# A fixed instruction order of a hybrid attention layer: half steps, evenly spaced scores, dense tiles dealt anew

## The chip, the cores and the metric

One core of a Trainium2 chip runs the whole layer in one launch. The metric is the device time of one execution in microseconds (us); 701.57 is the median of three for the kernel before (701.05 to 702.87).

## What is computed

One layer of a decoder on 512 prompt rows and 8 sample rows (one new token each, with 1024 cached rows in pages). The rows, modulated by an adaLN condition, are projected by `w_in` to all queries, keys, values and gates; two token mixers run on them, and their outputs are gated, projected up, merged, projected once more and normed. Cut to its core:

```python
h = x * (1.0 + scale) + shift
parts = split(h @ w_in)          # a_q a_kc a_vc a_ks a_vs a_kw a_vw a_g a_z b_q b_k b_v b_z m_a m_b
ck, cv = compress(k_cmp), compress(v_cmp)      # gelu(blk @ w1 + b1) @ w2 + b2, blocks of 32 rows, stride 16
o_a = g0 * attn(q, ck, cv) + g1 * attn(q, selected blocks) + g2 * attn(q, window of 512)   # NSA
o_b = attn(q, top 3 past blocks of 256 and the own block)                                 # MoBA
y_a = (o_a * silu(a_z)) @ w_up_a
y_b = (o_b * silu(b_z)) @ w_up_b
mixed = (sigmoid(m_a) * y_a + sigmoid(m_b) * y_b) @ w_out
x_new = layer_norm(alpha * x + gate * mixed)
```

The sample rows do the same over caches that a page table addresses: 64 pages each of the compression, selection and MoBA caches.

## The kernel before, in words

The projection by `w_in` is cut into **dense tiles** of 128 columns, named in `COLS` (q0 to q3 and bq0 to bq3 are queries, bk, bv, z, bz the other parts, `m0` to `m7` stand for the two tiles ma and mb of one merge gate). One tile (`dense`, line 538) loads a weight block of 512 KB, splits it into a high and a low part in two halves (ScalarE casts the high part, line 300; GpSimd or VectorE subtracts it, line 217; each half one step ahead of its use), and runs 48 matmuls of 260 columns into two PSUM banks called `d`. In the trace `d` is such a tile, `hl` a split weight, `raw` a loaded block, `s` a bank of scores, `p` probabilities, `pt` their transposes in PSUM, `pp` these copied back, `o` attention outputs, `e` the decode branch's bank.

The stages follow each other like this. To 52 us the adaLN condition and the first columns. Then the compression network of prompt and samples (`phi_prompt`, `phi_pair`, ends near 155 us; `u` its inputs, `gl` its gelu, line 781), with the tiles of `FILLS[0]` between; `dec_cmp`, the compression branch of the samples, with `CMP_FILLS` (to 170). Then the **prompt's attention**, eight pairs of heads (`attend`, pi = 0 to 7, 174 to 524 us), mixed with the samples' other branches (`dec_a`, `dec_b`) and with `FILLS[1]` to `FILLS[8]`; a stage with the rest of the samples' work and `FILLS[9]` (to 590); and the up and output projections with the norm.

The order is written by the kernel itself. Each of these works is a generator that yields an estimated cost; `merge` always steps the one with the smallest share of its total done. The totals are `ATT` (attention of a pair), `DEC_SHARE` and `DEC` (how far the samples' branches shall be behind each pair) and `fill_cost`. Where `behind[0]` is set, TensorE keeps exactly the order in which its instructions are written (`in_turn` ties each to the one before); the other engines are ordered by the tile scheduler, which honours `tc.high_priority()`.

One step of the attention handles one head's job (`step`, line 1111) as a list: for k = 0 to 3 a score of 512, 384, 256 or 128 columns (`score`), then a transposition of an earlier job (`turn`), at k = 1 the value product (`value`). A score is two matmuls and then a chain over three engines: VectorE adds the band and takes the extremum (1031, 1033), ScalarE takes the exponential (1036), VectorE the reciprocal (1037), GpSimd scales the probabilities (1038). Two banks `s` exist, so the third score waits for the first one's exponential. Items yield their estimated cost, so a step's scores stand as close together as the shares allow; a dense tile yields after every 12 matmuls.

The samples' branches read their caches through the ring `C` of two buffers (`CRAW = 2`) of 1 MB: the selection keys `slck` and MoBA's `mobk`, `mobv` page by page on SyncE's queue (line 729: read a page number, then one DMA), and the selection values `slcv` by two indirect DMAs a buffer on GpSimd (line 1160), 512 KB each.

Of the kernel before, what the change touches and what calls it, by code (L numbers as in the profile page):

```python
# [35 lines left out]
FILLS = [["ks", "vs", "ag", "vw", "q0", "kw", "q1", "q2", "q3"],  # L36
         ["bq1", "m0", "m1"],
         ["bk0", "bv0", "m2"],
         ["z0", "m3"],
         ["bv1", "z1", "m4"],  # L40
# [3 lines left out]
         ["bz1", "m5"],  # L44
         ["bz2", "m6", "g0", "g1", "bz3", "g2", "g3", "m7"]]
CMP_FILLS = ["bq2", "bq0", "bq3"]
DEC_SHARE = [0.13, 0.26, 0.39, 0.51, 0.57, 0.63, 0.765, 0.87]
DEC, DEC_PACE = 55100.0, 0.78
PHIS = 49353.58399999998
ATT = [17100] * 4 + [7100] * 3 + [11000]  # L50
# [113 lines left out]
def build(tc, A):  # L164
# [16 lines left out]
    def in_turn(i):  # L181

        D["pe"] = i
        if behind[0]:
            if behind[1] is not None:
                order(i, behind[1])
            behind[1] = i
        return i
# [33 lines left out]
    with ExitStack() as es:  # L222
# [315 lines left out]
        def dense(name, M=128):  # L538
# [3 lines left out]
            for hf in range(8 // per_u):  # L542
                hl = W.use()
                for bk in range(2):
                    for kk in range(per_u):
                        k = hf * per_u + kk
                        for j, (x, hb) in enumerate(((0, hTh), (1, hTh), (0, hTl))):
                            mm(acc[bk][:M, :HB], hl[:, x, kk * M:kk * M + M], hb[:, k, bk * HB:bk * HB + HB],
                               k == 0 and j == 0, k == 7 and j == 2)
                    if posts and (hf or bk):  # L550
                        posts.pop(0)()
                    yield per_u * 333
# [469 lines left out]
        def score(j, i):  # L1022
            n = 128 * i + 128
            s = p_s()
            for k in range(2):
                mm(s[:, :n], j.q2[k][:, i * 128:i * 128 + 128], j.kd[:, :n], k == 0, k == 1)
            sm = at.tile([128, 4], F32, name="sm", bufs=8)
# [10 lines left out]
            nc.gpsimd.tensor_scalar(pr, pr, sm[:, 3:4], j.gate(i), op0=OP.mult, op1=OP.mult)  # L1038
            return 2 * max(107, 0.42 * n)

        def turn(j, gi):
# [5 lines left out]
            if COPY_ENG[gi] == "a":  # L1047
                j.copied[gi] = nc.scalar.copy(t[:, :n], p[:, :n])  # L1048
            else:
                j.copied[gi] = nc.vector.tensor_copy(t[:, :n], p[:, :n])  # L1050
            return 109 * len(GRP[gi])
# [3 lines left out]
        def value(js):  # L1055
# [14 lines left out]
            return 160 + 1.7 * 1280 + (900 if last and pi < 4 else 0)  # L1070

        def finish(j):
            nc.scalar.mul(y[:, j.pi, :T], cur["o"], 0.5)
            return 1

        def cmp_score(r):
# [21 lines left out]
            return 8 * 200  # L1098

        def cmp_turn(r):  # L1100
# [6 lines left out]
            return 436  # L1107
# [3 lines left out]
        def step(j, extra=()):  # L1111

            extra = list(extra)
            b, a1, a0 = pipe
            seq = []
            for k in range(4):
                if j is not None:
                    seq.append((score, j, 3 - k))
                if b is not None and k:
                    seq.append((turn, b, k - 1))  # L1120
                if k == 1 and a1 is not None and a1.g:
                    seq.append((value, (a0, a1)))
                    if a1.last:
                        seq.append((finish, a1))
                if extra and k == 2:
                    f, arg = extra.pop(0)
                    seq.append((f, arg))
            pipe[:] = [j, b, a1]
            for f, *args in seq:
                yield f(*args)  # L1130
# [26 lines left out]
        def slcv_item(i):  # L1157
            def fn(t):
                for k in range(2):
# [42 lines left out]
        def dec_a():  # L1202

            xs = de.tile([128, 1026], F32, name="xs", tag="x")
# [150 lines left out]
        for pi in range(8):  # L1355
            fl = Flow(fills(FILLS[pi + 1]), fill_cost(FILLS[pi + 1]))
            if pi == 0:

                for _ in range(4):
                    fl.step()  # L1360
            merge(Flow(attend(pi), ATT[pi]), Flow(part(DEC_SHARE[pi]), max(1.0, (DEC_SHARE[pi] - done) * DEC)), fl)
            done = DEC_SHARE[pi]
        at_es.close()

# [8 lines left out]
        behind[:] = False, None  # L1373
# [375 lines left out]
```

## Time and profile before

| | us |
|---|---|
| median of the runs (701.05 to 702.87) | 701.57 |
| the profiled execution | 704.4 |
| its span, first to last instruction | 702.6 |
| TensorE busy (89% of the span) | 625.0 |
| VectorE, ScalarE, GpSimd busy | 322.9, 297.5, 288.4 |

The granted clock of TensorE is 0.938 of full speed over the span, and the DMA queues move 123.73 MB. TensorE is the busiest engine by far in every stage but the first, so a stage is read by what keeps TensorE idle, and by the clock that it was granted; busy time of the other engines counts only where TensorE waits for it.

### The profile page before, as it was taken

Reading aid. Unit: us, or ns where it says so; the run is one execution under the profiler, and the core shown is the slowest. Engines: PE = TensorE matmul, PEld = TensorE weight load, DVE = VectorE, ACT = ScalarE, POOL = GpSimd, SP = SyncE. Lnnn points to the kernel's source line nnn. Section 1 sums busy time; section 2 is a strip of 40 time slices with the busy share of each in tenths; the row PEclk is TensorE's granted clock in tenths of the full one; section 3 lists DMA queues with packets and bytes.
Section 4 is the critical chain, followed back from the end, with each engine's and each line's share of the span. In section 5 each row is a group of like instructions: output and inputs, shape, how many; then the busy total and the mean of one; then the engine's idle time right before and its main releaser. Section 6 shows DMA issues by size and latency. Waiting matters only on the chain. (4 is left out here: it accounts for less than half of the span.)

```text
span 702.6 us, 13239 instructions
## 1 busy us (share of the span) xinstructions
PE 625.0 (89%) x4709; PEld 519.6 (74%) x4709; DVE 322.9 (46%) x817; ACT 297.5 (42%) x678; POOL 288.4 (41%) x327
## 2 busy tenths in 40 slices
PE   5989999579599899999997898898989789999993
PEld 2788999579488767676675778775757569899773
DVE  3474365316655714734461636462321034655167
ACT  3375465325264635544451635452422142433422
POOL 2043847315253224434353535242402035566556
PEclk9999999689699999999998999989999879999997
DMA  8984476204447555666572653418779753244303
GB/s 313 393 304 140 139 196 181 61 30 126 130 140 260 202 158 173 210 226 213 165 244 71 225 203 113 136 37 281 234 240 304 269 203 105 72 150 132 139 1 122
DMA packets 63524, 123.73 MB, mean 176 GB/s; under 512 B 8354, under 2 KB 26594, under 8 KB 62946
## 3 DMA queue, kind: packets, MB, share of 16 engines
q1 hardware_dynamic: 62050, 118.69, 51.5%
q0 software_dynamic: 1408, 4.20, 1.8%
q8 instruction: 37, 0.61, 0.3%
q14 instruction: 29, 0.24, 0.1%
HBM read 113.81 MB, written 9.05 MB: 175 GB/s over the span
## 5 line engine op out<-in xcount | busy, mean ns | idle before, releaser
L172 PE MATMUL d<-hTh,hl 128*128 128x260 f32 (+1 forms) x1408 | 278.9, 296 | 6.7 <-ACT hl L300 4.9
L172 PEld LDWEIGHTS d<-hTh,hl 128*128 128x128 f32 (+1 forms) x1408 | 225.9, 195 | 29.1 <-issue 17.3
L172 PE MATMUL d<-hTl,hl 128*128 128x260 f32 (+1 forms) x704 | 204.4, 290 | 0.0
L172 PEld LDWEIGHTS d<-hTl,hl 128*128 128x128 f32 (+1 forms) x704 | 136.7, 194 | 0.5
L217 POOL TENSOR_TENSOR hl<-raw,hl 128x512 fp32r<-128x512 f32 x56 | 73.6, 1314 | 140.6 <-ACT hl L300 125.6
L300 ACT CAST hl<-raw 128x512 fp32r<-128x512 f32 (+1 forms) x111 | 68.0, 615 | 95.9 <-PE d L172 86.0
L217 DVE TENSOR_TENSOR hl<-raw,hl 128x512 fp32r<-128x512 f32 (+1 forms) x55 | 51.5, 936 | 75.8 <-ACT hl L300 67.8
L1036 ACT ACTIVATE p<-s,sm 128x512 f32<-128x512 f32 (+1 forms) x96 | 50.6, 528 | 53.8 <-DVE sm L1033 43.2
L1038 POOL TENSOR_SCALAR p<-p,sm,gp 128x512 f32<-128x512 f32 (+1 forms) x64 | 40.1, 630 | 78.0 <-DVE sm L1037 75.0
L191 PE MATMUL pt<-cst,p 128*128 128x128 f32 x240 | 40.8, 286 | 14.8 <-POOL p L1038 9.8
L172 PE MATMUL d<-yh,hl 128*128 128x260 f32 x256 | 46.3, 282 | 0.0
L191 PEld LDWEIGHTS pt<-cst,p 128*128 128x128 f32 x240 | 28.3, 146 | 22.5 <-POOL p L1038 11.9
L1033 DVE CUSTOM_DVE_ANT_0 s<-s,band 128x256 f32<-128x256 f32 (+1 forms) x48 | 17.4, 364 | 58.7 <-PE s L172 45.5
L172 PE MATMUL s<-kd,q 128*128 128x512 f32 (+1 forms) x96 | 36.4, 379 | 6.8 <-ACT p L1036 5.9
L172 PEld LDWEIGHTS d<-yh,hl 128*128 128x128 f32 x256 | 39.7, 188 | 1.1 <-issue 0.4
L1038 POOL TENSOR_SCALAR p<-p,sm,cst 128x512 f32<-128x512 f32 (+3 forms) x32 | 20.0, 626 | 40.9 <-DVE sm L1037 37.0
L172 PE MATMUL s<-u,w1h 128*128 128x256 f32 (+1 forms) x160 | 32.4, 298 | 4.1 <-ACT u L800 1.8
L172 PE MATMUL d<-yl,hl 128*128 128x260 f32 x128 | 36.0, 282 | 0.0
L172 PEld LDWEIGHTS s<-kd,q 128*128 128x128 f32 x96 | 19.2, 200 | 22.2 <-ACT p L1036 8.3
L172 PE MATMUL s<-kd,qx 128*128 128x512 f32 (+1 forms) x96 | 32.6, 339 | 0.0
L175 PE MATMUL o<-pp,v 128*64 128x384 f32 (+3 forms) x168 | 31.8, 448 | 0.0
L1048 ACT COPY pp<-pt 128x512 f32<-128x512 f32 (+1 forms) x48 | 23.0, 479 | 20.7 <-PE pt L191 20.3
(414 smaller groups left out, 1154.5 us busy)
## 6 DMA issues: line engine op xcount, KB each, us to landing
raw<-w_cols SPq DMA_DIRECT2D x46, 512.0 KB, 5.5
raw<-mobk SPq DMA_DIRECT2D x64, 256.0 KB, 3.9
raw<-mobv SPq DMA_DIRECT2D x64, 256.0 KB, 4.3
craw<-cmp SPq DMA_DIRECT2D x64, 128.0 KB, 2.7
u<-ada_ss SPq DMA_DIRECT2D x12, 512.0 KB, 9.1
raw<-slck SPq DMA_DIRECT2D x64, 64.0 KB, 2.0
raw<-ada_g SPq DMA_DIRECT2D x8, 512.0 KB, 4.2
raw<-w_up SPq DMA_DIRECT2D x8, 512.0 KB, 4.4
```

The source lines that it names most:

```text
L172: i = mmraw(out, lhsT, rhs, start=start, stop=stop, skip_group_check=True)
L175: i = mmraw(out, lhsT, rhs, start=start, stop=stop, skip_group_check=True)
L191: return in_turn(nc.tensor.transpose(out, x, unit))
L217: (nc.gpsimd if eng == "p" else nc.vector).tensor_sub(out, x, f32(hi))
L300: nc.scalar.copy(h, src)
L1033: nc.vector.tensor_tensor_reduce(out=s[:, b:n], in0=s[:, b:n], in1=j.band[:, 256 - (n - b):], scale=1.0, scalar=top, op0=OP.add, op1=OP.mi ...
L1036: nc.scalar.activation(pr, s[:, :n], AF.Exp, scale=-1.0, bias=sm[:, 1:2], accum_out=sm[:, 2:3])
L1038: nc.gpsimd.tensor_scalar(pr, pr, sm[:, 3:4], j.gate(i), op0=OP.mult, op1=OP.mult)
L1048: j.copied[gi] = nc.scalar.copy(t[:, :n], p[:, :n])
```

## The change

- `FILLS`: bq2, bq0 and bq1 go to the compression network's stage (three tiles more there); `CMP_FILLS` now holds bq3, bk0, bv0; m6 goes from the last stage to the attention's last pair. The attention has 26 tiles instead of 27, the last stage 4 instead of 6. `ATT`, `DEC`, `DEC_SHARE`, `DEC_PACE` get other numbers; the first pair's fill is run for 8 steps ahead instead of 4, each half as long.
- `dense` yields after every 6 matmuls instead of 12.
- `step` has four slots, each one score, one transposition and what else belongs there, and each slot yields the same cost, 1000.
- The chain behind a score (`probs`) and the copy of transposes get high priority.
- `slcv` gathers are issued only after the latest scaling of probabilities on GpSimd (`D["pool"]`).
- `dec_a` loads its first two buffers ahead.
- The fixed order ends with the attention; afterwards TensorE's instructions only stand behind the attention's last one (`floor`), and the scheduler orders them.

```diff
-FILLS = [["ks", "vs", "ag", "vw", "q0", "kw", "q1", "q2", "q3"],
-         ["bq1", "m0", "m1"],
-         ["bk0", "bv0", "m2"],
-         ["z0", "m3"],
-         ["bv1", "z1", "m4"],
+FILLS = [["ks", "vs", "ag", "vw", "q0", "bq2", "kw", "q1", "q2", "q3", "bq0", "bq1"],
+         ["m0", "m1"],
+         ["m2", "m3"],
+         ["z0", "bv1", "m4"],
+         ["z1", "m5"],
...
-         ["bz1", "m5"],
-         ["bz2", "m6", "g0", "g1", "bz3", "g2", "g3", "m7"]]
-CMP_FILLS = ["bq2", "bq0", "bq3"]
-DEC_SHARE = [0.13, 0.26, 0.39, 0.51, 0.57, 0.63, 0.765, 0.87]
-DEC, DEC_PACE = 55100.0, 0.78
+         ["bz1", "m6"],
+         ["bz2", "g0", "g1", "bz3", "g2", "g3", "m7"]]
+CMP_FILLS = ["bq3", "bk0", "bv0"]
+DEC_SHARE = [0.155, 0.28, 0.405, 0.53, 0.59, 0.645, 0.74, 0.855]
+DEC, DEC_PACE = 57600.0, 0.85
-ATT = [17100] * 4 + [7100] * 3 + [11000]
+ATT = [16000] * 4 + [8000] * 3 + [10400]
...
         D["pe"] = i
+        if "floor" in D:
+            order(i, D["floor"])
...
-                    if posts and (hf or bk):
-                        posts.pop(0)()
-                    yield per_u * 333
+                        if kk % 2 == 1:
+                            if posts and (hf or bk) and kk == per_u - 1:
+                                posts.pop(0)()
+                            yield 666
...
+            with tc.high_priority():
+                probs(j, i, n, s)
+
+        def probs(j, i, n, s):
...
-            nc.gpsimd.tensor_scalar(pr, pr, sm[:, 3:4], j.gate(i), op0=OP.mult, op1=OP.mult)
-            return 2 * max(107, 0.42 * n)
+            D["pool"] = nc.gpsimd.tensor_scalar(pr, pr, sm[:, 3:4], j.gate(i), op0=OP.mult, op1=OP.mult)
...
-            extra = list(extra)
             b, a1, a0 = pipe
-            seq = []
-            for k in range(4):
+            slots = [[] for _ in range(4)]
+            for k, seq in enumerate(slots):
                 if j is not None:
-                    seq.append((score, j, 3 - k))
+                    seq.append(lambda i=3 - k: score(j, i))
                 if b is not None and k:
-                    seq.append((turn, b, k - 1))
-                if k == 1 and a1 is not None and a1.g:
-                    seq.append((value, (a0, a1)))
-                    if a1.last:
-                        seq.append((finish, a1))
-                if extra and k == 2:
-                    f, arg = extra.pop(0)
-                    seq.append((f, arg))
+                    seq.append(lambda i=k - 1: turn(b, i))
+            if a1 is not None and a1.g:
+                slots[1].append(lambda: value((a0, a1)))
+                if a1.last:
+                    slots[1].append(lambda: finish(a1))
+            for f, arg in extra:
+                slots[2].append(lambda f=f, arg=arg: f(arg))
             pipe[:] = [j, b, a1]
-            for f, *args in seq:
-                yield f(*args)
+            for seq in slots:
+                for f in seq:
+                    f()
+                    yield (600 if j is None else 1000) / len(seq)
...
             def fn(t):
-                for k in range(2):
+                with tc.issue_after(D["pool"].ins):
+                  for k in range(2):
                     nc.gpsimd.indirect_dma_start(out=t[:, k * 1024:k * 1024 + 1024], out_offset=None, in_=A["slcv"],
...
         def dec_a():
 
+            C.load_to(1)
+            yield 2500
...
-                for _ in range(4):
+                for _ in range(8):
                     fl.step()
+                fl.total, fl.done = fl.total - fl.done, 0.0
...
         at_es.close()
+        behind[0] = False
+        D["floor"] = D["pe"]
...
-        behind[:] = False, None
+        D.pop("floor")
```

**TensorE, within the attention of one pair.** Before, a score of 512 columns, one of 384 and a transposition of four stand together (`s_3354`, `s_3364`, `pt_3374`):

```order
L172 MATMUL s_3354<-kd_1627,q2_2141 128x512
L172 MATMUL s_3354<-kd_1627,qx_2142 128x512
L172 MATMUL s_3364<-kd_1627,q2_2141 128x384
L172 MATMUL s_3364<-kd_1627,qx_2142 128x384
L191 MATMUL pt_3374<-cst0_72,p_3308 128x128
L191 MATMUL pt_3374<-cst0_72,p_3263 128x128
L191 MATMUL pt_3374<-cst0_72,p_3159 128x128
L191 MATMUL pt_3374<-cst0_72,p_3116 128x128
L172 MATMUL d_3278<-hTh_73,hl_3282 128x260 x2
L172 MATMUL d_3278<-hTl_74,hl_3282 128x260
```

In the changed order such three items, now with dense matmuls between score and score (`s_3410`, its 512 columns, stands six more rows of `d_3424` above this piece) and between score and transposition:

```order
L172 MATMUL d_3424<-hTh_73,hl_3328 128x260 x2
L172 MATMUL d_3424<-hTl_74,hl_3328 128x260
L172 MATMUL s_3443<-kd_1649,q2_2341 128x384
L172 MATMUL s_3443<-kd_1649,qx_2342 128x384
L172 MATMUL d_3425<-hTh_73,hl_3328 128x260 x2
L172 MATMUL d_3425<-hTl_74,hl_3328 128x260
L172 MATMUL d_3425<-hTh_73,hl_3328 128x260 x2
L172 MATMUL d_3425<-hTl_74,hl_3328 128x260
L193 MATMUL pt_3459<-cst0_72,p_3365 128x128
L193 MATMUL pt_3459<-cst0_72,p_3324 128x128
L193 MATMUL pt_3459<-cst0_72,p_3278 128x128
L193 MATMUL pt_3459<-cst0_72,p_3256 128x128
```

A quarter of a dense tile's work, 12 or 6 matmuls, now separates each item from the next.

**GpSimd, at the second pair of gathers.** Before, both gathers of the pair stand behind a weight split, wherever the scheduler found room:

```order
L217 TENSOR_TENSOR hl<-raw,hl 128x512
L1160 DMA raw<-slcv,vidx 128x1024 x2
L1038 TENSOR_SCALAR p<-p,sm,gp 128x512
L1038 TENSOR_SCALAR p<-p,sm,gp 128x384
L993 TENSOR_TENSOR qx<-y,q_4209 64x512
L1038 TENSOR_SCALAR p<-p,sm,gp 128x256
L1038 TENSOR_SCALAR p<-p,sm,gp 128x128
```

With the change each pair stands right behind a scaling of probabilities; the first and the second pair come within one job's four scalings, with the `qx` split (which waits for the first pair's landing) between:

```order
L1045 TENSOR_SCALAR p<-p,sm,gp 128x512
L1160 DMA raw<-slcv,vidx 128x1024 x2
L1045 TENSOR_SCALAR p<-p,sm,gp 128x384
L1045 TENSOR_SCALAR p<-p,sm,gp 128x256
L996 TENSOR_TENSOR qx<-y,q_4404 64x512
L1045 TENSOR_SCALAR p<-p,sm,gp 128x128
L1160 DMA raw<-slcv,vidx 128x1024 x2
L1045 TENSOR_SCALAR p<-p,sm,gp 128x512
```

**TensorE, where the second of these pairs is read.** The score of 128 columns whose scaling (the last `p` 128x128 above) releases the gathers, and the read `e<-raw,tp` of what they bring:

```order
L172 MATMUL s<-kd,q_3719 128x128
L172 MATMUL s<-kd,qx 128x128
L172 MATMUL e<-vnew,np 128x128 x2
L172 MATMUL d<-hTh,hl 128x260 x2
L172 MATMUL d<-hTl,hl 128x260
L172 MATMUL d<-hTh,hl 128x260 x2
L172 MATMUL d<-hTl,hl 128x260
L193 MATMUL pt<-cst_72,p 128x128 x2
L172 MATMUL e<-raw,tp 32x128
L175 MATMUL e<-raw,tp 32x128 x31
```

Between the score and the read stand two products of the new rows, six dense matmuls and two transposes. At the fourth pair it is six dense matmuls alone.

In the changed order the four reads of `slck` (`e<-raw,zn`) stand 27, 24 and 26 rows apart on TensorE, where before it was 29, 49 and 47; 24 dense matmuls, three scores, twelve transposes and one read lie between the first and the second.

## Rows read from the trace of the kernel before

**Rows 1.** Windows by stage: us of the stretch, busy time (instructions) of each engine, clock, DMA share, GB/s.

```profile
120.00:160.00 40.00, 27.41 (x184) 26.33 (x183) 11.36 (x22) 11.48 (x26) 11.13 (x13) 0.74 0.17 48
160.00:200.00 40.00, 32.29 (x221) 28.49 (x221) 22.68 (x68) 16.52 (x40) 15.97 (x18) 0.83 0.45 131
200.00:520.00 320.00, 292.27 (x2290) 230.50 (x2288) 149.65 (x471) 150.38 (x384) 125.68 (x149) 0.96 0.57 187
520.00:587.00 67.00, 59.62 (x433) 47.14 (x426) 15.97 (x16) 17.80 (x36) 18.92 (x18) 0.90 0.69 234
```

**Rows 2.** TensorE's waits: line waited for, us in total, times, longest us.

```profile
PE pt L172 <- ACT gl L781: 10.5, 2, 6.2
PE pt L191 <- POOL p L1038: 9.8, 7, 4.2
...
PE s L172 <- ACT p L1036: 7.2, 6, 2.1
...
PE d L172 <- ACT hl L300: 4.9, 2, 3.4
...
PE d L172 <- POOL hl L217: 1.8, 2, 1.0
```

**Rows 3.** Timeline of TensorE at 128 us, columns: start, us, what [idle before <- releaser].

```profile
128.05 0.58 PE L172 MATMUL pt<-gl,w2h 128*128 128x256 f32 x1 [6.16 <-ACT gl L781]
```

**Rows 4.** Windows of two stretches at half clock in the compression stage.

```profile
124.30:138.00 13.70, 7.83 (x33) 7.39 (x34) 5.12 (x7) 3.73 (x8) 4.74 (x6) 0.50 0.28 77
144.80:151.60 6.80, 6.24 (x28) 6.24 (x29) 0.79 (x3) 1.13 (x3) 0.00 (x0) 0.50 0.00 0
```

**Rows 5.** Chain of waits, 544 to 560 and 612 to 617 us: start, us, what.

```profile
546.42 0.55 PE e L172
...
557.38 0.63 ACT hl L300
...
558.08 1.27 POOL hl L217
...
615.12 1.43 PE d L172 x12
```

**Rows 6.** Timeline, SyncE's queue and TensorE, at 177 and 181 us.

```profile
176.80 23.53 SPq L729 DMA_DIRECT2D raw<-slck  x37
...
180.80 1.03 PE L172 MATMUL e<-raw,zn 128*32 128x512 f32 x1 [5.59 <-DMA raw<-slck]
```

**Rows 7.** Timeline of all engines, 357 to 374 us.

```profile
357.00 0.28 PE L172 MATMUL s<-kd,qx 128*128 128x128 f32 x1
...
358.61 0.98 POOL L1038 TENSOR_SCALAR p<-p,sm,gp 128x256 f32<-128x256 f32 x2
...
371.04 1.26 POOL L993 TENSOR_TENSOR qx<-y,q 64x512 fp32r<-64x512 f32 x1 [5.38 <-DMA raw<-slcv,vidx]
...
373.44 1.11 PE L191 MATMUL pt<-cst,p 128*128 128x128 f32 x4 [4.23 <-POOL p L1038]
```

**Rows 8.** Windows of the five half-clock stretches of the attention, the first and the sum.

```profile
373.40:380.30 6.90, 6.86 (x28) 3.56 (x32) 1.11 (x4) 0.00 (x0) 1.41 (x2) 0.51 0.00 0
...
sum 23.90, PE 23.47 PEld 15.05 DVE 7.95 ACT 3.93 POOL 5.24; mean PE 4.69 PEld 3.01 DVE 1.59 ACT 0.79 POOL 1.05
```

**Rows 9.** Instructions of line 1160, the gathers: duration ns, and us to landing.

```profile
L1160 POOL DMA_INDIRECT raw<-slcv,vidx x8: 944/1026/1301, 354.7 to 391.3; - x8
...
DMA to landing us min/median/max: 4.2/6.0/7.8
```

**Rows 10.** Windows, 520 to 560 us; DMA issues: count, KB each, us to landing.

```profile
520.00:540.00 20.00, 19.28 (x152) 14.19 (x145) 2.23 (x4) 4.78 (x10) 2.22 (x2) 0.99 0.80 260
540.00:560.00 20.00, 15.83 (x124) 11.35 (x122) 2.03 (x2) 3.89 (x8) 2.99 (x4) 0.94 0.84 295
...
raw<-mobv SPq DMA_DIRECT2D x64, 256.0 KB, 4.3
...
raw<-ada_g SPq DMA_DIRECT2D x8, 512.0 KB, 4.2
```

More of the change, by code (lines that the diff above doesn't have):

```diff
@@ L1046, in turn @@
             t = j.pt[gi] = at.tile([128, n], F32, name="pp", tag=f"pp{gi}", bufs=(3, 2, 2)[gi])
[L1047 to L1051, printed above, removed]
+            with tc.high_priority():
+                j.copied[gi] = (nc.scalar.copy if COPY_ENG[gi] == "a" else nc.vector.tensor_copy)(t[:, :n], p[:, :n])
         cur = {}
@@ L1069, in value @@
                         mm(cur["o"][OWN[g]], cv2[:, g], cur["pc", pi], False, True)
-            return 160 + 1.7 * 1280 + (900 if last and pi < 4 else 0)
         def finish(j):
             nc.scalar.mul(y[:, j.pi, :T], cur["o"], 0.5)
-            return 1
         def cmp_score(r):
@@ L1097, in cmp_score @@
             cur["c"] = c
-            return 8 * 200
         def cmp_turn(r):
@@ L1106, in cmp_turn @@
             cur["pc", r] = pc
-            return 436
         pipe = [None, None, None]
         def step(j, extra=()):
-            extra = list(extra)
             b, a1, a0 = pipe
-            seq = []
-            for k in range(4):
+            slots = [[] for _ in range(4)]
+            for k, seq in enumerate(slots):
                 if j is not None:
-                    seq.append((score, j, 3 - k))
+                    seq.append(lambda i=3 - k: score(j, i))
                 if b is not None and k:
-                    seq.append((turn, b, k - 1))
-                if k == 1 and a1 is not None and a1.g:
-                    seq.append((value, (a0, a1)))
-                    if a1.last:
-                        seq.append((finish, a1))
-                if extra and k == 2:
-                    f, arg = extra.pop(0)
-                    seq.append((f, arg))
+                    seq.append(lambda i=k - 1: turn(b, i))
[5 more added lines that the diff above has]
+                slots[2].append(lambda f=f, arg=arg: f(arg))
             pipe[:] = [j, b, a1]
-            for f, *args in seq:
-                yield f(*args)
+            for seq in slots:
+                for f in seq:
+                    f()
+                    yield (600 if j is None else 1000) / len(seq)
         def attend(pi):
```

## The prediction, made before the changed kernel ran

> **What bounds the kernel now.** I read the windows by stage first [rows 1]. TensorE is busy 27.41 of 40 us from 120 to 160 us (the end of the compression network), 32.29 of 40 from 160 to 200, 292.27 of 320 in the attention proper, and 59.62 of 67 in the stage behind it. The reader should see two losses in each row: idle time (40 - 27.41 = 12.6 us in the first) and the granted clock, 0.74 in that row and 0.83 in the next, where the engine does the same matmuls at 1.2 GHz, half its 2.4 GHz. All of TensorE's matmuls are the same before and after, so the sum is one of idle time and of half clock alone. Then the list of TensorE's waits [rows 2]: the network's second product waits 10.5 us for a gelu, in two pieces; transposes wait 9.8 us for the scaled probabilities and scores wait 7.2 us for the exponential that frees their bank. The weight splits that feed the dense tiles cost it only 4.9 + 1.8 us. Last, single places in the timeline, below. The profiled execution (704.4 us, span 702.6) is 2.8 above the median of the runs, 701.57; the sum is made in the span and the difference is put on the median.
>
> **The gelu waits.** The stall that ends at 128.05 [rows 3] has no dense matmul in front of it: the nine tiles dealt to this stage are used up. The stretches behind the two stalls ran at half clock, with 7.83 and 6.24 us of work in them [rows 4], which at full clock would be 7.0 less. So 12.6 + 7.0 = 19.6 us are there to be won. The change deals three more tiles here; a tile is 48 matmuls, twelve take 1.43 us [rows 5], so 5.7 a tile and 17.2 together, which leave the attention (one tile) and the last stage (two). Their own time is no gain or loss; what they fill is. They are spread by shares, not put at the waits, and the order shows the second gelu product still among the network's own matmuls. I take -15; bounds -18 and -8 (only the first stall and its slow stretch filled).
>
> **Pages of the selected branch.** The first read of that cache stalls 5.59 us at 180.80 [rows 6]. SyncE issues the pages one by one: 37 in 23.53 us, 0.64 each, so a buffer of 16 takes 10.2. In the changed order the first read comes after more work (about 14 us behind the last compression product, where 13 us are needed), so that stall goes, with the idle time and half clock of 160 to 200: 7.7 us, and 2 x 0.17 x 40 = 13.6 us at half clock, some 5 lost. But between the four reads there stand now 24 dense matmuls (2.9 us), three scores (0.7), twelve transposes (four take 1.11 at half clock [rows 7], so 1.7) and the read (0.55 [rows 5] and a little): 5.9 us, against the 10.2 that SyncE needs, since only two buffers exist. Three stalls of 3 to 5 us, 13 us, and some 4 of half clock: 17 against 12.7 saved, **+4**. Bounds -6 (spread by the waits that stay anyway) and +13.
>
> **Scores.** Two scores back to back need two banks, and the next waits for the exponential; a transposition then meets probabilities of a chain that is not done. The slot form puts a quarter of dense work between scores, and the priority puts the chain ahead of weight splits. A score of 128 columns ends at 357.28, and its scaled probabilities, two tiles in one row, are there at 359.6 [rows 7], so one takes some 2.0 us. In the changed order a transposition stands some 4 us of TensorE's work behind its score. So the 9.8 + 7.2 us of waits [rows 2] and about 3 of waits for copies should go, 20 us of the 27.7 idle in 200 to 520. Behind such stalls stand slow stretches: 23.9 us with 23.47 of work in five places [rows 8], 11.7 us lost, of which I give 8 to these stalls. **-28**; bounds -35 (all idle time and most of the clock) and -14 (half).
>
> **The gathers.** This is the one place where the order speaks against the change. The value pages of the selected branch come by gathers on GpSimd, which land 4.2 to 7.8 us after issue, median 6.0, and hold the engine 1.03 us each [rows 9]. Before, the scheduler put them wherever GpSimd had room, ahead of their use as the order shows, and once they did harm even so: GpSimd's qx split waited 5.38 us for a landing, and probabilities queued behind it held TensorE for 4.23 [rows 7]. Now each pair is tied behind the newest probability scaling, and TensorE's read stands only two matmuls of the new rows, six dense ones and two transposes (1.3 us) behind that score; at the second place six dense ones (0.7). The scaling ends 2.0 us after the score, the second gather follows its sister by 1.0 and lands 6.0 later: 9.0 us. TensorE stands 9.0 - 1.3 = 7.7 and 9.0 - 0.7 = 8.3 us, 16 in all, and two slow stretches of 6.9 us behind them [rows 8] cost 3.4 each: **+22**. Bounds: 0 (other work keeps TensorE late, so the data are there), and +33 (7.8 us to landing, and twice the slow stretch). The Trainium skill, DMA: Bandwidth & Descriptors, section Anatomy of one DMA, SWDGE path, fits 2.0 us plus bytes over 436e3 per DMA, 3.2 us for these 512 KB; the trace's shortest is 4.2, so the measurement decides. By the page the two stalls would be 4.9 and 5.5 and the sum 683 instead of 688.5. The same page, section Rules for kernel authors, says to issue a DMA early and to wait late, which is against tying it to the latest score; the 5.38 us in rows 7 agree.
>
> **The last stage.** From 520 to 587 us 234 GB/s ran [rows 1], 67 x 0.234 = 15.7 MB: half of the 64 loads of MoBA values and the gates' weights [rows 10]. Two dense tiles leave, 11.4 us of cover: 67 - 11.4 = 55.6 are left. The most that the trace shows here is 295 GB/s at a DMA share of 0.84 [rows 10], by which 15.7 MB take 53 us; so the transfers, hidden until now, come to bound the stage. The order set free lets the scheduler fill some waits. I take +2; bounds -4 and +8 (260 GB/s, which the 20 us before show [rows 10], make 60.4). **The up projections** start behind a stage that idles more, so part of them at half clock: +2, bounds 0 and +4.
>
> The eight head steps instead of four, the new shares and the planner's constants only set where tiles fall; the order holds their whole effect, which is priced above. The earlier load at the decode branch's start fills a buffer that is free then, hidden behind the dense tiles; without that cover it would be 10.2 us of page issue. The m6 tiles' write to memory moves into the attention, onto SyncE's queue among the loads: a put waits for its tile's activation, and loads queue behind it; that is in the pacing's bound.
>
> Sum: -15 + 4 - 28 + 22 + 2 + 2 = -13. Span 689.6; on the median 701.57 - 13 = **688.5**.
>
> **Rivals.** (A) The gathers and pages are there in time. For it: everything behind a late TensorE gets slack, and one stall pays for the next. Against: the 1.3 us distance. It gives 688.5 - 22 - 4 = 662. Chance 0.22.
> (B) Slower: the score chain's priority starves the weight splits. A split is a cast of 0.63 us on ScalarE and a subtraction of 1.27 us on GpSimd (or one on VectorE) [rows 5]; put behind probabilities and, on GpSimd, behind the qx that waits for a gather, it comes late, and TensorE stands at a half tile's first matmul, as it did for 4.9 + 1.8 us [rows 2]. The attention has 52 halves. One subtraction late on each would be 52 x 1.27 = 66; it decides from 13/52 = 0.25 us a half, where the gain is gone. At 0.5 us a half the time is 714. For it: GpSimd now carries the scaling first. Against: the splits stand one half ahead, and the present waits of this kind are four in number. Chance 0.15.
> (C) Transfers bound the last two heads and the last stage at 260 GB/s instead of 295, with m6's weights drawn into the same stretch: +5 there and as much in the last heads: 700. Chance 0.13.
> (D) The change does not do what it says: the scheduler keeps the old spacing. The order shows the scores apart on TensorE, so only the priority could be idle: then half of the -28 is lost, 702. Chance 0.05.
> The forecast has the other 0.45, by its own errors 675 to 701.
>
> **How the numbers follow.** A measurement of this kernel can tell about 0.3% from no change, 2.1 us: faster is below 699.5, slower above 703.7. A and nearly all of the forecast lie below, with half of C: 0.77. B and the high ends of the pacing and gather bounds lie above: 0.17. Left for no change: 0.06. Both ends of the six terms together would span 638 to 739; that all err one way is not to be expected, and their errors added as squares give some 25 us each way. The range takes in A with its own spread and the foot of B: 655 to 706.
>
> **What would show it.** Right: in the changed profile the dense matmuls lie in front of the gelu waits and the clock of that stretch is above 0.9; waits of transposes and scores for probabilities fall from 17 us to below 5; new waits of the branch reads on the gathers, two of 5 us and more, and on the pages, three of 3 to 5; the last stage about 58 us with a DMA share near 0.8. Wrong: no wait on a gather (A), or waits of dense matmuls on splits above 13 us in sum (B).

## The result, and the profile after

The changed kernel takes 694.64 us (median of 692.0 to 696.31) against 702.22 for the kernel before in the same runs: ratio 0.9883, interval 0.9838 to 0.9927, so 7.6 us (1.2%) faster. The forecast was 688.5, a gain of 13, in a range of 655 to 706. The profiled execution of the changed kernel is its fastest run, 692.0 with a span of 690.2 and a granted clock of 0.953; the other three ran at 0.942 to 0.944 and took 694.2 to 696.3. Between the two profiled spans lie 12.4 us, and the readings below are made in these. In the experiments one run of 675.74 us (the last one on pages, whose other four took 665.6 to 668.28) and one of 709.46 us of the kernel before ran at a lower clock than the rest and are left out of the comparisons.

First the windows of [rows 1] again, for the changed kernel (us of the stretch, busy time of TensorE, its loads, VectorE, ScalarE, GpSimd; clock, DMA share, GB/s):

```profile
120.00:160.00 40.00, 40.00 (x349) 39.77 (x349) 14.61 (x29) 17.73 (x41) 15.96 (x17) 1.00 0.31 98
160.00:200.00 40.00, 34.29 (x273) 31.12 (x272) 25.45 (x73) 18.93 (x44) 16.61 (x19) 1.00 0.50 154
200.00:520.00 320.00, 283.69 (x2237) 227.20 (x2237) 147.30 (x467) 148.18 (x380) 123.73 (x147) 0.94 0.57 184
```

From 120 to 160 us TensorE has no idle time left (40.00 of 40, it was 27.41) and the clock is 1.00. From 200 to 520, where the tied gathers and the pages are read, it is busy 283.69 instead of 292.27 at a lower clock: this stage did not win. The stretches hold other work than before, so here are the windows cut at the same places of the program, which are the first `slck` read, the last value product and the first up projection. Before:

```profile
0.00:180.80 180.80, 151.02 (x1211) 138.12 (x1211) 86.68 (x183) 82.46 (x171) 73.46 (x87) 0.93 0.58 189
180.80:523.90 343.10, 312.73 (x2402) 245.47 (x2402) 158.09 (x506) 157.90 (x406) 131.87 (x158) 0.94 0.56 182
523.90:589.80 65.90, 59.04 (x432) 48.64 (x431) 16.66 (x17) 18.43 (x37) 18.92 (x18) 0.90 0.70 236
589.80:702.60 112.80, 102.21 (x670) 87.34 (x668) 61.51 (x111) 38.70 (x64) 64.11 (x65) 0.96 0.31 103
```

and after:

```profile
0.00:189.20 189.20, 172.13 (x1417) 159.32 (x1417) 95.18 (x207) 91.32 (x194) 80.86 (x95) 0.99 0.60 194
189.20:521.60 332.40, 293.99 (x2314) 234.47 (x2313) 151.93 (x486) 153.19 (x393) 126.27 (x151) 0.94 0.57 184
521.60:574.30 52.70, 44.48 (x312) 32.57 (x313) 7.26 (x11) 10.96 (x22) 8.53 (x12) 0.87 0.77 278
574.30:690.20 115.90, 103.21 (x670) 87.70 (x668) 65.94 (x114) 41.51 (x70) 71.70 (x70) 0.97 0.31 104
```

The counts in the TensorE column are its matmuls. 206 more now stand ahead of the first read (three tiles are 144; most of the others are dense matmuls too, which stood behind that read before), 88 fewer in the attention, 120 fewer in the last stage. At 1.43 us for twelve [rows 5] that is 24.5 us of work in, 10.5 and 14.3 out. The stages' lengths changed by +8.4, -10.7, -13.2 and +3.1 us. So the first part gained 16.1, the attention 0.2, the last stage lost 1.1 and the projections lost 3.1: 12.1 of the 12.4. Small differences of this kind say little: in two kernels below that change nothing ahead of the first read (the one without the tie, and the one with the last stage's order fixed) that part took 191.2 and 193.2 us, where it is 189.2 here.

The list of TensorE's waits says why the attention gave nothing. Its columns are the line that waited and what it waited for, us in total, times, and the longest:

```profile
PE e L172 <- DMA raw<-slcv,vidx: 21.3, 2, 10.9
PE e L172 <- DMA raw<-slck: 11.1, 3, 5.2
...
PE d L193 <- DVE v L600: 3.5, 1, 3.5
PE d L172 <- ACT hl L302: 2.8, 1, 2.8
...
PE pt L193 <- ACT pp L1054: 1.5, 2, 0.8
...
PE d L172 <- POOL hl L219: 1.4, 2, 0.8
...
PE pt L193 <- DVE pp L1054: 0.7, 2, 0.5
```

The waits for probabilities, 9.8 and 7.2 us in [rows 2], are no longer in the list, and copies of transposes cost 1.5 + 0.7. In their place stand two waits for gathers, 21.3 us, and three for pages, 11.1. The waits for weight splits fell to 2.8 + 1.4, so the weight splits were not starved.

### The profile page after: what moved, and what is told of

Same layout as the page of the kernel before. It is cut to its first block, busy times and chain, and to the rows that moved or that the text cites. A ratio compares the mean times of both kernels' runs of the same rounds, so it can differ in the third digit from the quotient of the medians.

```text
span 690.2 us, 13240 instructions
## 1 busy us (share of the span) xinstructions
PE 613.8 (89%) x4709; PEld 514.0 (74%) x4709; DVE 320.3 (46%) x817; ACT 297.0 (43%) x678; POOL 287.4 (42%) x327
## 4 chain that ended last, share of the span: by engine, by line
PE 69%; DMA 9%; DVE 6%; issue 5%; SPq 4%; POOL 4%; ACT 3%; POOLq 0%; DVEq 0%; ACTq 0%
PE d L172 39%; PE s L172 11%; PE e L172 6%; PE pt L193 3%; SPq L732 3%; PE o L172 3%; PE o L175 3%; DMA raw<-slcv,vidx 2%; DMA raw<-mobv 2%; PE pt L172 2%; PE e L175 1%; DMA u<-ada_ss 1%; POOL hl L219 1%; DMA m_d<-mg 1%; DMA craw<-cmp 1%
## 5 line engine op out<-in xcount | busy, mean ns | idle before, releaser
L172 PE MATMUL d<-hTh,hl 128*128 128x260 f32 (+1 forms) x1408 | 282.0, 296 | 4.6 <-ACT hl L302 2.8
L172 PEld LDWEIGHTS d<-hTh,hl 128*128 128x128 f32 (+1 forms) x1408 | 223.3, 192 | 33.4 <-issue 22.8
L172 PE MATMUL d<-hTl,hl 128*128 128x260 f32 (+1 forms) x704 | 202.2, 288 | 0.0
L172 PEld LDWEIGHTS d<-hTl,hl 128*128 128x128 f32 (+1 forms) x704 | 134.8, 191 | 1.1 <-issue 0.8
L219 POOL TENSOR_TENSOR hl<-raw,hl 128x512 fp32r<-128x512 f32 x54 | 70.9, 1313 | 74.2 <-ACT hl L302 60.7
L219 DVE TENSOR_TENSOR hl<-raw,hl 128x512 fp32r<-128x512 f32 (+1 forms) x57 | 53.3, 936 | 48.3 <-ACT hl L302 47.3
L172 PE MATMUL e<-raw,tp 128*32 128x512 f32 (+1 forms) x40 | 20.5, 598 | 25.6 <-DMA raw<-slcv,vidx 21.3
L1038 DVE TENSOR_REDUCE sm<-s 128x1 f32<-128x256 f32 (+1 forms) x48 | 17.0, 355 | 52.4 <-PE s L172 50.9
L219 POOL TENSOR_TENSOR u<-craw,u 128x512 fp32r<-128x512 f32 x16 | 22.1, 1389 | 29.5 <-ACT u L839 29.5
L172 PE MATMUL s<-kd,q 128*128 128x512 f32 (+1 forms) x96 | 32.8, 342 | 0.0
```

The costliest lines, as they stand in the source:

```text
L172: i = mmraw(out, lhsT, rhs, start=start, stop=stop, skip_group_check=True)
L219: (nc.gpsimd if eng == "p" else nc.vector).tensor_sub(out, x, f32(hi))
L1038: nc.vector.tensor_reduce(sm[:, 0:1], s[:, :b], axis=AX, op=OP.min)
```

## The experiments

All times are compared with the kernel before, which took 701.6 to 702.2 us in these sessions; each ratio has its interval behind it. "The changed kernel" is 694.6.

### The gathers' tie undone

```diff
-                with tc.issue_after(D["pool"].ins):
-                  for k in range(2):
+                for k in range(2):
                     nc.gpsimd.indirect_dma_start(out=t[:, k * 1024:k * 1024 + 1024], out_offset=None, in_=A["slcv"],
```

> The changed kernel with one part undone: the slcv gathers are no longer tied behind the latest probability scaling on GpSimd. Theory (the tie makes the two waits of TensorE on gathers, 21.3 us in the profile of the changed kernel, and two stretches of half clock of 13.7 and 10.2 us behind them): the order now puts the second pair of gathers four scalings earlier and the fourth pair four scalings earlier, so the waits fall to 0 to 6 us together and the time to about 676 us (670 to 682). Rival (the gathers are slow wherever they stand, and GpSimd's qx split, which waits for their landing, then holds the probabilities back as in the kernel before, where that cost 4.2 us on TensorE): the wait only changes its name to one on p, and the time stays at 688 to 697.

Measured: 671.14 us (668.88 to 673.31), 0.9565 (0.9505 to 0.9625). This one line cost the changed kernel 23.5 us by the medians (22.3 by the two ratios), and the waits fell as the theory said. To see why, the timeline of GpSimd in the changed kernel (start, us, what, idle time before and who ended it):

```profile
357.06 1.06 POOL L1160 DMA_INDIRECT raw<-slcv,vidx  x1 [0.30 <-issue]
358.43 0.96 POOL L1160 DMA_INDIRECT raw<-slcv,vidx  x1 [0.30 <-issue]
...
365.28 1.26 POOL L996 TENSOR_TENSOR qx<-y,q 64x512 fp32r<-64x512 f32 x1 [2.19 <-DMA raw<-slcv,vidx]
366.64 0.45 POOL L1045 TENSOR_SCALAR p<-p,sm,gp 128x128 f32<-128x128 f32 x1
367.41 1.04 POOL L1160 DMA_INDIRECT raw<-slcv,vidx  x1 [0.31 <-issue]
368.75 0.95 POOL L1160 DMA_INDIRECT raw<-slcv,vidx  x1 [0.30 <-issue]
...
399.78 1.26 POOL L996 TENSOR_TENSOR qx<-y,q 64x512 fp32r<-64x512 f32 x1 [2.77 <-ACT qx L995]
401.14 0.45 POOL L1045 TENSOR_SCALAR p<-p,sm,cst 128x128 f32<-128x128 f32 x1
```

and of TensorE:

```profile
360.52 0.28 PE L172 MATMUL s<-kd,qx 128*128 128x128 f32 x1
...
373.47 0.39 PE L172 MATMUL e<-raw,tp 128*32 128x128 f32 x1 [10.89 <-DMA raw<-slcv,vidx]
...
396.98 0.27 PE L172 MATMUL s<-kd,qx 128*128 128x128 f32 x1
...
408.40 0.42 PE L172 MATMUL e<-raw,tp 128*32 128x128 f32 x1 [10.38 <-DMA raw<-slcv,vidx]
```

The score that the second pair is tied to ends at 360.80. Its scaling (`p`, 128x128) starts only at 366.64: ahead of it in GpSimd's order stands the `qx` split, which waits for the landing of the first pair (issued at 357.06 and 358.43). The second pair goes out at 367.41 and 368.75, lands 4.5 and 4.6 us later, and TensorE has stood still since 362.58. At the second place the score ends at 397.25 and its scaling starts only at 401.14, again behind a `qx`. The profile puts this `qx`'s wait down to ScalarE's cast for the same tile; the third pair landed at nearly the same time, so which of the two held it is open. The clock falls to half during each stall and stays there for some 5 us of work behind it:

```profile
365.60:379.30 13.70, 5.83 (x72) 5.29 (x73) 0.89 (x3) 0.00 (x0) 3.37 (x4) 0.50 0.32 95
403.10:413.30 10.20, 4.90 (x70) 4.29 (x71) 0.00 (x0) 0.00 (x0) 0.94 (x1) 0.50 0.39 111
```

There 5.83 and 4.90 us of work ran at 1.2 GHz, so 5.4 us were lost. Without the tie, in the same place:

```profile
359.03 1.03 POOL L1159 DMA_INDIRECT raw<-slcv,vidx  x1
360.36 0.94 POOL L1159 DMA_INDIRECT raw<-slcv,vidx  x1 [0.30 <-issue]
...
367.13 0.27 PE L172 MATMUL e<-raw,tp 128*32 128x128 f32 x1 [2.44 <-DMA raw<-slcv,vidx]
...
390.48 0.30 PE L172 MATMUL e<-raw,tp 128*32 128x128 f32 x1
```

The second pair is issued at 359.03 and 360.36, 8.4 us earlier, ahead of the scaling it was tied to; the wait at the first read is 2.44 us, at the other place there is none. The attention of this kernel, from its first `slck` read to its last value product, is 22.7 us shorter with the same 2314 matmuls:

```profile
191.20:500.90 309.70, 291.32 (x2314) 232.92 (x2313) 152.78 (x486) 153.13 (x393) 126.11 (x151) 0.96 0.61 197
```

The rival, that `qx` would then hold probabilities back and TensorE with them, failed: no wait for `p` is in this kernel's list. The Trainium skill, DMA: Bandwidth & Descriptors, section Rules for kernel authors, asks to issue a DMA early and wait late; the 23.5 us are the price of the contrary here.

### The tie kept, the loads moved ahead

```diff
+            C.load_to(C.nl)
             xo = D["xo"] = de.tile([128, 3, 128], F32, name="xo")
...
-            yield 300
+            yield 1300
...
+                if q == 0:
+                    C.load_to(C.nl)
                 yield 1400
```

The first load stands behind the last read of a MoBA key buffer, the second behind the first window value read; two later steps cost 500 less each.

> The changed kernel with the tie kept, but the second buffer of each pair is loaded one step of the decode branch earlier (right after the last read that frees its slot), with 1000 more of cost before the first read and 500 less at two later steps. Theory (the distance between the issue and the read is all that matters, not the tie itself): waits on gathers fall from 21.3 to below 5 us, time 672 to 682 us. Rival (the tie, or the qx split behind the gathers, costs by itself): waits on gathers fall, but waits of transposes and scores for probabilities rise by 5 us or more; time above 684.

Measured: 676.09 us (675.66 to 681.71), 0.9657 (0.959 to 0.9724). Its two waits in this place:

```profile
PE pt L193 <- POOL p L1045: 5.0, 2, 3.3
...
PE e L172 <- DMA raw<-slcv,vidx: 3.4, 1, 3.4
```

Distance alone brings 18.5 of the 23.5 us: the gather waits fall from 21.3 to 3.4. The 5.0 us for `p` are new, the rival's sign in part. In the first of the two waits (1.8 us) probabilities queue behind a `qx` that waits for a landing. In the second (3.3 us), after all four gathers of the last two pairs have gone out together, they queue behind a `qx` again; it starts as the last gather lands (8.4 us after issue), but the profile names a cast on ScalarE that ends at the same time, so there the landing is not shown to be the cause.

### The kernel before with the tie alone

```diff
+            D["pool"] = nc.gpsimd.tensor_scalar(pr, pr, sm[:, 3:4], j.gate(i), op0=OP.mult, op1=OP.mult)
...
+                with tc.issue_after(D["pool"].ins):
```

> The kernel before with one part of the change alone: the slcv gathers tied behind the latest probability scaling. Theory (the tie costs by the distance between the tied scaling and the read, whatever the spacing): new waits of TensorE on gathers, 6 to 20 us in sum, time 708 to 722 against 701.6. Rival (the tie only costs together with the slots, since in the old order scores stand close together and well ahead of the read): waits below 5 us and 699 to 706.

Measured: 719.34 us (717.08 to 722.3), 1.0291 (1.0253 to 1.0328).

```profile
PE e L172 <- DMA raw<-slcv,vidx: 11.8, 2, 8.9
PE pt L191 <- POOL p L1038: 11.7, 6, 6.4
```

It is 17 us slower by the medians (20 by the ratio): 11.8 us of waits on gathers, and a wait for probabilities of 6.4 us where one of 4.2 was [rows 2]. The tie costs in either order. That the gather waits are 11.8 us here and 21.3 in the changed kernel can't be put down to the slots: with the slots undone in the changed kernel (below) they are still 21.4. Which other part of the change adds to them is open.

### Pages: the reads spread

```diff
             C.load_to(1)
-            yield 2500
+            yield 1300
...
-                    yield 1500
+                    yield 2400
```

(`DEC` 60000, shares raised to match.)

> The changed kernel with the four slck reads further apart: each costs 2400 instead of 1500 in the sharing, the step before the first 1300 instead of 2500, and the shares and the total are raised by the 2400 that this adds, so that all later steps keep their place. Theory (SyncE issues the 16 pages of a buffer in 10.2 us and TensorE comes too early): waits on slck fall from 11.1 to below 5 us, with 10.2 us of half clock near 209 to 226 us gone; time 8 to 13 us below that of the changed kernel, 682 to 687. Rival (the pages are issued late because something else stands in front of them on SyncE's queue, a weight load or a put that waits): the waits follow the reads wherever they stand, at least 8 us remain and the time is 691 to 696.

Measured: 689.68 us (688.9 to 691.11), 0.9831 (0.9776 to 0.9885). It overlaps with the changed kernel's interval, and the waits on `slck` are 9.1 us in four pieces instead of 11.1 in three. The changed kernel's SyncE queue and two of the reads show why spreading does little:

```profile
203.34 8.67 SPq L732 DMA_DIRECT2D raw<-slck  x15
...
214.13 4.30 SPq L732 DMA_DIRECT2D raw<-slck  x8
...
208.88 1.03 PE L172 MATMUL e<-raw,zn 128*32 128x512 f32 x1 [5.20 <-DMA raw<-slck]
...
220.78 1.03 PE L172 MATMUL e<-raw,zn 128*32 128x512 f32 x1 [4.66 <-DMA raw<-slck]
```

15 pages take 8.67 us, 0.58 each, back to back; the last of the 64 is out at 218.4 and the last read waits until 220.78. SyncE issues pages almost without a break from 182 us on, so the last read can't come much earlier, however the reads are spread; in this experiment it stood at 221.21, in the next at 221.89. The kernel before had its last page out at 211.3, since it issued 37 pages without a break from 176.8 on [rows 6]; so pages that start sooner might help, and so might more work of other kinds in front of the reads. No run tried the first. A later try without the tie, with 3300 for each read:

> The kernel without the tie (671.1 us) with the slck reads spread further: 3300 instead of 1500 for each, 1300 instead of 2500 before the first, total and shares raised by the 6000 that this adds. SyncE has its 64 pages out at about 220 us in every version so far, and the last read stands at 221 to 222. Theory (the waits go only if TensorE has that much other work in front of the reads): waits on slck fall from 9.4 to below 4 us, half clock near 210 to 226 us goes; 660 to 667 us. Rival (work drawn ahead is missing later, among the gathers and MoBA reads, and the wait comes up there): waits on slck fall, another rises by as much, 668 to 674.

Measured: 667.3 us (665.6 to 668.28), 0.9509 (0.9461 to 0.9556), with 10.0 us of waits on `slck` in its profiled execution (the one of 675.74 us). The waits did not go, against my theory; the median lies 3.8 us below that without spreading, and the intervals of the two ratios overlap. What the spreading is worth stays open.

### New FILLS alone on the kernel before

> The kernel before with one part of the change: the new FILLS and CMP_FILLS alone (three more dense tiles in the compression network's stage, one less in the attention, two less in the last stage); constants, steps, scores and gathers as before. Theory (dense tiles fill 12.6 us of idle time and give back some 7 of half clock, at no cost elsewhere): waits for gl fall from 10.5 to below 2 us, clock of 120 to 160 us above 0.95, time 12 to 18 us below the kernel before, 684 to 690. Rival (the idle time only moves: with fewer tiles in the attention and the last stage, score chains and MoBA's loads are no longer covered): the stage gains 15 but the later stages lose 5 to 15 of it, 690 to 702.

The edit is the `FILLS` and `CMP_FILLS` of the diff. Measured: 694.3 us (689.94 to 696.35), 0.9877 (0.9809 to 0.9945). The windows from 120 to 160 us, of the part up to the first read, of the attention and of the last stage:

```profile
120.00:160.00 40.00, 40.00 (x349) 39.77 (x348) 14.52 (x26) 17.67 (x40) 15.71 (x17) 1.00 0.34 104
...
0.00:190.10 190.10, 165.96 (x1360) 152.76 (x1361) 92.49 (x190) 88.46 (x185) 76.60 (x91) 0.95 0.58 192
190.10:521.80 331.70, 301.68 (x2349) 236.40 (x2349) 155.01 (x501) 155.09 (x400) 130.20 (x155) 0.96 0.57 186
521.80:578.70 56.90, 47.23 (x336) 36.00 (x335) 12.73 (x15) 14.64 (x29) 13.36 (x14) 0.88 0.74 260
```

The compression network's idle time is gone, as forecast; up to the first read the kernel has 149 matmuls more (17.8 us) and is 9.3 us later, 8.5 won. The last stage is 9.0 us shorter for 96 matmuls less, 11.4 us, so 2.4 are given back there, and its DMA rate rose from 236 to 260 GB/s. The attention is 11.4 us shorter for 53 matmuls less, 6.3 us, so 5.1 are won. The time is in the rival's range, but not by its account: what the later stages give back is less than the 5 to 15 us that it named, and the first part won 8.5 instead of 15. And with everything else of the change in place but the tie, the old tables:

> The kernel without the tie (671.1 us) with the old FILLS and CMP_FILLS. On the kernel before the new ones alone were worth 7.3 us, with 9.8 us of idle time won in the compression network, but stalls of other kinds left in the attention. Theory (the idle time and half clock of the compression stage is a price of its own, 15 us by the sum of the prediction): waits for gl of 10 us return, 683 to 689. Rival (a part of it is given back in the attention and the last stage, where the tiles then cover reads): 676 to 680.

Measured: 674.59 us (668.53 to 677.43), 0.9612 (0.9535 to 0.9688), against 671.14 with the new ones. The gelu waits are back in full,

```profile
PE pt L172 <- ACT gl L784: 10.4, 2, 6.1
```

and still the time is only 3.5 us longer, which these runs do not separate from nothing. Counted by matmuls as above, between the two profiles, the new tables win 11.4 us up to the first read and lose 3.2 in the attention, 1.6 in the last stage and 3.4 in the projections. That the tiles which stand later under the old tables cover waits there fits this, but no run tests it.

### Slots undone

In the changed kernel `step` is the old list again, with the old `ATT`; priority, half steps, tiles and tie stay.

> The changed kernel with one part undone: a step of the attention is again the list of the kernel before, each item yielding its estimated cost (and the attention's totals ATT are the old ones), while the priority, the half steps, the tiles and the tie stay. Theory (it is the distance between scores, and between a score and the transposition of it, that took away the 17 us of waits for probabilities): waits of transposes and scores for p come back, 8 to 17 us in sum, with half clock behind them; time 8 to 20 us above the changed kernel, 703 to 715. Rival (the priority alone did it, the chain being late only because splits stood before it): those waits stay below 4 us and the time within 4 us of 694.6.

Measured: 697.84 us (695.58 to 701.24), 0.9957 (0.9925 to 0.9989), 3 us above the changed kernel, with intervals that just overlap. Its waits of this kind, with the pages' among them:

```profile
PE pt L193 <- DVE pp L1055: 5.3, 4, 2.0
...
PE e L172 <- DMA raw<-slck: 2.9, 1, 2.9
PE s L172 <- ACT p L1044: 2.7, 3, 1.7
PE pt L193 <- ACT pp L1055: 2.6, 4, 1.1
PE pt L193 <- POOL p L1046: 2.2, 3, 1.4
```

12.8 us of waits for `p` and `pp` are back, and the wait on pages fell from 11.1 to 2.9. One wait took the other's place; the sum of the two is 15.7 us against 13.3 (the changed kernel's 11.1, 1.5 and 0.7). The same on the kernel without the tie:

> The kernel without the tie (671.1 us) with the old list of a step's items and the old ATT. In the changed kernel this cost 3.2 us, with the gather stalls there. Theory (the gather stalls hid part of it, because the score chains that run on during a stall are not late any more): without them it costs 6 to 14 us, 677 to 685. Rival (the half steps of the dense tiles already give the distance): 2 to 5 us as before, 673 to 676.

Measured: 668.77 us (668.25 to 669.4), 0.9537 (0.949 to 0.9584), against 671.14 and 0.9565 with slots: no loss at all, both of my theories wrong. So with the old step the tie costs 29.1 us (697.84 to 668.77).

```profile
PE pt L193 <- DVE pp L1055: 5.3, 4, 2.5
...
PE pt L193 <- POOL p L1046: 3.3, 4, 1.3
...
PE pt L193 <- ACT pp L1055: 3.0, 4, 1.1
```

The transposes' waits are there (11.6 us), but of a score's wait for its bank, 7.2 us in [rows 2], only 0.8 came back, and the waits for pages and gathers fell, from 9.4 and 2.4 us with slots to 3.1 and nothing. Then the half steps undone, slots kept:

> The kernel without the tie (671.1 us) with dense tiles again stepped by 12 matmuls, and 4 head steps instead of 8; slots kept. Theory (six matmuls are enough to keep a score and the next apart, twelve leave some scores back to back, so some waits for p return): waits for p 4 to 9 us, 675 to 683. Rival (with slots the step's size is indifferent): 668 to 674.

Measured: 672.13 us (666.69 to 672.68), 0.9584 (0.9537 to 0.9631): the same within the interval, and no wait for `p` came back. So for the time neither the slots nor the half steps are needed when the other is there. That either of the two makes the distance between scores is what this suggests, but it is not shown: both undone together was not tried, nor were the new totals and shares alone.

### Priority and the last stage

Without the two `tc.high_priority()` blocks:

> The changed kernel without the high priority around the score chain and the copies of transposes. Theory (the slots are enough, 4 us of work stand between a score and its transposition): waits for p stay below 4 us, time 691 to 699. Rival (without priority weight splits and the decode branch's long vector work go ahead of the chain): waits for p or for pp of 6 us or more, time 700 to 710.

Measured: 692.62 us (691.66 to 694.27), 0.989 (0.9865 to 0.9916): no difference, no new wait. With the last stage's order fixed as written:

> The changed kernel with the order of the last stage fixed again as written (the kernel before does so), nothing else. Theory (the stage is bound by the transfers of MoBA values and gate weights, so the order within it matters little): last stage 51 to 57 us long against 52.7, time 693 to 700. Rival (the free order is what shortens the stage, by drawing dense matmuls into the waits for mobv): last stage 58 us or more, time 700 to 706.

Measured: 697.06 us (692.21 to 700.82), 0.9929 (0.9892 to 0.9965). The last stage in this kernel:

```profile
524.30:582.70 58.40, 45.79 (x313) 31.88 (x314) 8.90 (x12) 12.57 (x25) 11.27 (x13) 0.85 0.75 253
```

The stage took 58.4 us instead of 52.7, as the rival said, at 253 GB/s instead of 278; the time stays in the theory's range. In the median 2.4 us of it are left, inside the intervals.

## Why the prediction was right, step by step

The forecast's sum was -13 in the span; 12.4 were found there, and 7.6 between the medians. The profile is of the fastest run, so the nearness in the span is in part luck.

**The gelu waits (-15), with the first page wait.** Right in kind, somewhat over-sized. Up to the first read 16.1 us were won, where this term and the 5.6 us of the first page wait made 20.6. A new wait of 3.5 us at 179.59, of a transposition for the copy of the values `v` out of its bank, is of the size of most of the difference. From 160 to 200 us the half clock went as forecast (0.83 to 1.00), but of the 7.7 us of idle time there 5.7 are left. That what is filled here is a gain was right inside the stage, but not shown for the kernel as a whole: undone alone, it costs 3.5 us, inside the intervals.

**Pages (+4).** Right: three waits, 11.1 us, where "three stalls of 3 to 5 us, 13 us" stood; they were 1.27, 5.20 and 4.66, with 3.12 and 4.82 us of work at half clock behind the last two (from 208.6 and 218.8 us), so 4.0 lost where "some 4" stood.

**Scores (-28).** The waits went as said: 17 us of them left the list. Without the tie the attention won 22.9 us (33.4 shorter, 10.5 of that by matmuls that moved), where this term with the 17 us of pages and the 5 us of half clock behind the first page wait made 16 (-28 + 17 - 5); so its size was at least reached. But the reason given, the slots and the priority, is not shown: the priority does nothing measurable, the slots are not needed for the time when the half steps are there, and with 11.6 us of the transposes' waits back it is no longer. Which part of the change took the time away is open.

**The gathers (+22).** Right in place and kind, under-sized: "7.7 and 8.3 us" were 10.89 and 10.38. The step that failed was "The scaling ends 2.0 us after the score": it stood behind `qx` on GpSimd and ended 6.3 us after it (360.80 to 367.09), at the second place 4.3 (397.25 to 401.59). Against that the gathers that TensorE waited for landed sooner than the 6.0 us reckoned with, 4.6 and 5.3 us after issue, and TensorE reached the first read 1.8 us behind the score, not 1.3. I had seen GpSimd's queue in [rows 7] and priced it only as a thing of the past. With the half clock the two stalls cost 21.3 + 5.4 = 26.7 us in the profile, and 23.5 in the runs; a wait of 2.4 us is left without the tie. The Trainium skill's fit (DMA: Bandwidth & Descriptors, section Anatomy of one DMA), 3.2 us a gather by the prediction's estimate, would have made the stalls shorter still; the eight gathers of the changed kernel landed after 4.3 to 6.7 us, none as fast as that.

**The last stage (+2) and the projections (+2).** Measured +1.1 and +3.1, differences too small to read. The stage was 52.7 us long, not 58: 120 matmuls left it where two tiles are 96, and it moved 14.7 MB (52.7 x 0.278), not 15.7, which the sum had kept although the two tiles' weights leave as well. Its DMA rate rose from 236 to 278 GB/s, as a stage that transfers bind would show; but with the order fixed it took 58.4 us at 253 GB/s, so transfers alone do not set its length.

**The rivals.** (A) is the kernel without the tie: 671 us, where 662 were worked out for gathers and pages both in time; the pages still cost 9.4 us of waits there, and the gathers 2.4. (B) fell: waits for splits went down. (C) did not come: the last value product ends at 521.6, 2.3 us earlier, and the last stage ran at 278 GB/s, not 260; its sum, 688.5 and twice 5, is 698.5, where 700 was written. (D) was right that the priority is idle, but that costs nothing. The upper end of the six terms together is 737.6, not 739.

The sum is the rest of two large terms of opposite sign, and both were priced near. Without the tie the forecast's other terms leave -35 in the span, and 34.4 us were found (702.6 to 668.2); the tie, +22, cost 22.0 between the spans and 23.5 between the medians. Inside the -35 luck helped: that kernel won 14.1 us up to the first read, less than the 20.6 forecast, and 22.9 in the attention, more than the 16. So the change wins 31 us (702 to 671) and throws away 23.5 of them in one line. What wins the 31 us is shown by stage and by the waits that went, not by part of the change: of the parts that were undone one at a time, none but the tie moves the median by more than 3.5 us.

## What to carry to other kernels

When a DMA is tied to an event, write down how far its reader stands behind that event in the reader's own queue, and how late the issuer comes to the DMA because of what stands in front of it there. If the reader's distance is less than the issuer's delay and the landing time together, the tie is a stall of the difference, and here work at half clock came behind it. At the first place: 6.3 to the end of the scaling, 1.7 to the second gather, 4.6 to its landing, less the reader's 1.8, makes 10.8 us, and 10.89 were measured. Undo the parts of a change in pairs as well as one at a time: here the slots and the half steps may each have stood in for the other, and undoing one told nothing of the pair. Of the kernels run, the changed one without the tie (671.1, also 667.3 with wider page reads and 668.8 with the old step) beats both kernels by 3 to 5%; these three are not told apart.

## What was not expected

A split that has nothing to do with the gathers (`qx`) waited on GpSimd for their landing in both kernels (5.38 us in [rows 7], 2.19 after); why its order asks for that I have not found out. And TensorE's waits trade places: with 10.4 us of gelu waits back, or 11.6 us of the transposes' waits, the time moved by only 3.5 and -2.4 us.
